# First pair of a ConvGLU as ordinary products, its operand sums in place, and the last four blocks in one down product

## The chip, the cores and the metric

The kernel runs on one core of a Trainium2 chip. The core has a matrix engine (TensorE; PE in the profile, its weight loads PEld), a vector engine (VectorE, DVE), a scalar engine (ScalarE, ACT), a general engine (GpSimd, POOL) and a sync engine (SyncE, SP) that here only issues transfers. Each engine takes its instructions from a queue of its own, in order. The metric is the device time of one execution in microseconds (us); lower is better. Before the change the median of three runs is 2178.03 us (2174.79 to 2182.94).

## The reference

One transformer encoder layer is applied to two requests that share the weights: a prompt of 1024 tokens and a sample of 512 tokens, each behind 16 learned meta tokens. The width D is 1024. All inputs and outputs are 32-bit floats.

```python
h = x + mixer(rms_norm(x))            # two kinds of attention heads, then w_out
n = rms_norm(h)                       # over the width, with a gain
gate = n @ w_ff_gate                  # 1024 x 2816
gate = pad[:, :-2] * conv_w[0] + pad[:, 1:-1] * conv_w[1] + pad[:, 2:] * conv_w[2] + conv_b   # over the tokens
h = h + (gelu(gate) * (n @ w_ff_up)) @ w_ff_down      # 2816 x 1024
y = rms_norm(h)[:, N_META:]
```

The change concerns the last three lines for the prompt (the ConvGLU and the final norm). The 2816 inner columns are 22 blocks of 128, and the kernel takes them two at a time, as 11 pairs.

## The kernel before

**Arithmetic.** Every product is made from three matmuls of a reduced float format (`mm3`, L129 to L133): an operand is split into a high part, rounded by ScalarE, and a low part, the difference, made by VectorE or GpSimd (`split`, L125 and L126); the three matmuls are high by high (L131), high by low (L132) and low by high (L133). All activations lie transposed, with the width on the 128 partitions and the tokens along the free dimension, so `h` is 8 tiles `h[:, k]`, one for each 128 of the width.

**Stages.** The program runs the projections, the attention of both requests, the sample's ConvGLU, and the prompt's output projection (`mixer_out`); the prompt's ConvGLU (`prompt_glu`) comes last, alone. Its matmuls begin at about 1417 us of the profile and it takes the remaining 760 us.

**The halves.** `prompt_glu` cuts the 1024 tokens into a left and a right half (H = 512 tokens, with a column of halo at each end: W = 514) and the width into an upper half (k = 0 to 3) and a lower half (k = 4 to 7). This gives four quarters of the normed input: b11 and b21 (left tokens), b12 and b22 (right tokens). A pair of gate or up blocks is then a 2 by 2 product of half matrices, and it is done with seven products in place of eight, by Strassen's method in Winograd's form (`products`, with `ORDER = 1, 2, 6, 7, 4, 5, 3`). Product 1 takes b11, 2 takes b21, 3 takes b22, and products 4 to 7 take sums of quarters: t1 = b12 - b11 (product 5), t2 = b22 - t1 (product 6), t3 = b22 - b12 (product 7) and t4 = b21 - t2 (product 4). These sums of the activations are made once, in the first pair, and each is split into a high and a low part (`put`). The weights of a pair need their own sums and splits each time (`strassen_weights`): two raw tiles come by transfers on SP's queue (L821), VectorE makes four sums in place (L836 to L841, one of them in a temporary `s`), ScalarE casts the seven high parts and GpSimd makes the seven low parts. The halves of the split weights are handed out in turn (`Halves`) from three pairs of tiles of 1024 columns (`w_hi`, `w_lo`, NW = 3); a tile is free again when the products of both of its halves are done. The raw tiles `w_f` are two (NRAW = 2).

**A pair.** The gate's seven products have 2 x 258 columns, and their results are combined on VectorE out of PSUM (L900); `gate_out` makes the convolution (L941, two VectorE steps L944) and the GELU (L946). The up's seven products have 512 columns; `up_out` multiplies by the gate (L953) and splits the result into `a_hi` and `ga` (the low part lies in a `ga` block). `down_all` multiplies the two blocks of the pair by `w_down` and adds the result to `h` on VectorE (L986): 8 width blocks by 2 halves of the tokens, each of six matmuls of 512 columns.

**The first pair.** When it begins, only the tokens of the first two of three chunks have their norm's factor `rstd`; the sum of squares of the last chunk is still being made on GpSimd (L619). So the first pair's gate is made of ordinary products (`dense`), left half first; the matmul that averages the last chunk's squares (L1011) follows behind the first of them, then `rstd` is finished, the right quarters are normed (L882) and split, and the right half of the gate follows. The sums t1 to t4 are then made from quarters that are normed once more into temporaries `tmp` (five buffers): 12 norms and 16 subtractions, a half of these on GpSimd (L886). The up's seven products follow. The first pair's gate weights are split with GpSimd's help (`load_weight` with `nc.gpsimd`).

**The end.** The last pair's down product is done in four chunks of 256 tokens: for each width block six matmuls of 256 columns, an add to `h` (L1096), a square (L618) and an add to the chunk's sum of squares on GpSimd (L619). While the next chunk runs, the chunk's mean is made by a matmul (L624), then `rs`, and `h` is scaled (L1083 on VectorE, L1080 and L1081 for each fourth) and stored. The last chunk sums its squares on TensorE (L1100) instead.

**What sets the order.** The program is traced in the order of the code, and a planner (`schedule_with_timeline_sim`) then orders each engine's queue by a simulated time line: an instruction that the simulation finds ready goes ahead of an earlier one that it finds waiting. A tile of a rotating tag waits until a buffer of the tag is free, and a tile of a later pool waits for the tiles whose memory it takes over.

## Time and profile before

| | before |
|---|---|
| median of three runs | 2178.03 us (2174.79 to 2182.94) |
| the profiled execution's own time | 2178.3 us |
| its span, first to last instruction | 2176.5 us |
| TensorE busy | 2062.9 us, 95% of the span |
| VectorE, ScalarE, GpSimd busy | 67%, 50%, 41% |
| mean granted TensorE clock | 0.981 |

The profile is one execution. "Busy" is the time in which an engine has an instruction under way; matmuls overlap each other, so that a row's duration (0.28 us for 258 columns) is more than the distance from one start to the next, and the distance is what a stream of matmuls costs. A row of the time line has the start, the duration, the engine, the line of the code, the operation, output and inputs, the shape and the number of merged instructions; in brackets stands how long the engine stood idle before it and what released it. A row of the windows has, for a stretch of time, the busy time and the number of instructions of each engine, the granted TensorE clock (1.00 is full speed), the share of the transfer engines and what they moved.

### The profile page before, as it was taken

The page shows a single profiled execution, that of the slowest core. Times are in us where ns is not written, and L with a number is a line of the kernel's source. Part 1 is how long each engine was busy: PE and PEld are TensorE (multiplying, and loading weights), DVE is VectorE, ACT ScalarE, POOL GpSimd, SP SyncE. Part 2 cuts the span into 40 slices and gives each one's busy share as a digit, 9 for nine tenths or more (in the row PEclk, how much of TensorE's full clock was granted, in tenths as well). Part 3 has the DMA queues.
Part 4 walks back from the last instruction along what each step waited for, and adds up shares of the span by engine and source line. Part 5 has one row for each costly group of instructions (what it writes and reads, how often), then busy time and mean ns, then how long its engine had stood idle before and what let it go on. Part 6 is the DMA issues. An engine that isn't in the chain of part 4 may idle for free.

```text
span 2176.5 us, 33391 instructions
## 1 busy us (share of the span) xinstructions
PE 2062.9 (95%) x12598; PEld 1853.3 (85%) x12598; DVE 1457.5 (67%) x2345; ACT 1083.4 (50%) x1970; POOL 900.2 (41%) x678
## 2 busy tenths in 40 slices
PE   7999999998999999999999999967999999999996
PEld 7898989986897888898889988965888888888885
DVE  7745565677758767667777777776665665666655
ACT  5534544567747445577777646532333222233333
POOL 5753345310132222344444313466544444445444
PEclk9999999999999999999999999988999999999998
DMA  6763455554233222233332227501111111111112
GB/s 228 223 214 111 140 166 161 166 188 130 73 89 91 86 78 82 87 104 101 124 108 77 70 75 242 169 29 39 59 59 49 49 46 52 58 39 59 58 40 78
DMA packets 112544, 222.84 MB, mean 102 GB/s; under 512 B 14464, under 2 KB 65920, under 8 KB 111872
## 3 DMA queue, kind: packets, MB, share of 16 engines
q1 hardware_dynamic: 92800, 149.40, 21.3%
q10 hardware_dynamic: 19584, 71.31, 10.0%
q8 instruction: 99, 1.62, 0.3%
q14 instruction: 61, 0.50, 0.1%
HBM read 172.11 MB, written 48.55 MB: 101 GB/s over the span
## 4 chain that ended last, share of the span: by engine, by line
PE 78%; DVE 9%; ACT 3%; POOL 3%; issue 3%; DMA 1%; ACTq 0%; DVEq 0%; POOLq 0%
PE ps_d L132 10%; PE ps_d L133 10%; PE ps_d L131 9%; PE ps_mm L131 9%; PE ps_mm L132 9%; PE ps_mm L133 9%; PE ps_t L466 5%; PE ps_s L445 3%; PE ps_s L446 3%; PE ps_o L481 2%; DVE p L449 2%; PE ps_o L480 1%; POOL w_lo L126 1%; DVE tmp L882 1%; PE ps_s L132 1%
## 5 line engine op out<-in xcount | busy, mean ns | idle before, releaser
L126 POOL TENSOR_TENSOR w_lo<-w_f,w_hi 128x512 fp32r<-128x512 f32 (+1 forms) x185 | 293.9, 1601 | 334.1 <-ACT w_hi L125 333.1
L131 PE MATMUL ps_mm<-xhi,w_hi 128*128 128x258 f32 (+4 forms) x1232 | 396.6, 322 | 2.6 <-DVE hn L117 2.5
L132 PE MATMUL ps_mm<-xlo,w_hi 128*128 128x258 f32 (+4 forms) x1232 | 392.1, 318 | 0.0
L133 PE MATMUL ps_mm<-xhi,w_lo 128*128 128x258 f32 (+4 forms) x1232 | 390.1, 317 | 0.0
L125 ACT CAST w_hi<-w_f 128x512 fp32r<-128x512 f32 (+1 forms) x219 | 160.4, 755 | 364.5 <-PE ps_d L132 279.1
L449 DVE TENSOR_SCALAR_CACHE_REDUCE p<-ps_s 128x1044 f32<-128x1044 f32 (+7 forms) x212 | 223.1, 1052 | 91.3 <-PE ps_s L446 76.5
L125 ACT CAST pt_hi<-ps_t 128x512 fp32r<-128x512 f32 (+8 forms) x360 | 170.3, 483 | 189.2 <-PE ps_t L466 174.1
L452 ACT ACTIVATE p<-p,nm 128x1040 f32<-128x1040 f32 (+7 forms) x212 | 215.2, 1015 | 92.0 <-DVE p L449 91.3
L131 PEld LDWEIGHTS ps_mm<-xhi,w_hi 128*128 128x128 f32 x1232 | 234.6, 191 | 12.9 <-DVE hn L117 3.1
L126 DVE TENSOR_TENSOR pt_lo<-ps_t,pt_hi 128x512 fp32r<-128x512 f32 (+6 forms) x312 | 172.8, 563 | 107.0 <-ACT pt_hi L125 106.0
L132 PEld LDWEIGHTS ps_mm<-xlo,w_hi 128*128 128x128 f32 x1232 | 234.4, 190 | 9.1 <-issue 0.5
L133 PEld LDWEIGHTS ps_mm<-xhi,w_lo 128*128 128x128 f32 x1232 | 234.4, 190 | 8.5 <-issue 0.2
L445 PE MATMUL ps_s<-k,q 128*128 128x348 f32 (+6 forms) x552 | 177.8, 328 | 17.8 <-DVE p L449 16.9
L900 DVE TENSOR_TENSOR tmp<-ps_d,tmp 128x512 f32<-128x512 f32 (+1 forms) x147 | 99.4, 687 | 133.5 <-PE ps_d L133 133.3
L466 PE MATMUL ps_t<-ident,p 128*128 128x128 f32 (+10 forms) x1188 | 181.9, 268 | 0.6 <-ACT r_rows L501 0.3
L446 PE MATMUL ps_s<-k,q 128*128 128x348 f32 (+6 forms) x552 | 170.7, 316 | 0.0
L466 PEld LDWEIGHTS ps_t<-ident,p 128*128 128x128 f32 (+10 forms) x1188 | 141.5, 135 | 29.4 <-issue 4.1
L151 POOL CAST w_hi<-w_f 128x1024 fp32r<-128x1024 f32 x66 | 70.8, 1081 | 218.0 <-issue 88.5
L986 DVE TENSOR_TENSOR h<-ps_d,h 128x1024 f32<-128x1024 f32 x80 | 97.7, 1222 | 85.7 <-PE ps_d L133 85.7
L132 PE MATMUL ps_d<-ga,w_hi 128*128 128x512 f32 x320 | 126.9, 397 | 0.9 <-POOL ga L126 0.9
L133 PE MATMUL ps_d<-a_hi,w_lo 128*128 128x512 f32 x320 | 126.8, 396 | 0.0
L445 PEld LDWEIGHTS ps_s<-k,q 128*128 128x128 f32 (+5 forms) x552 | 100.2, 182 | 31.0 <-DVE p L449 27.7
(312 smaller groups left out, 5462.2 us busy)
## 6 DMA issues: line engine op xcount, KB each, us to landing
w_f<-w_in ACTq DMA_DIRECT2D x36, 512.0 KB
w_f<-w_out ACTq DMA_DIRECT2D x32, 512.0 KB
q<-qk SPq DMA_DIRECT2D x48, 257.0 KB
w_f<-w_gate ACTq DMA_DIRECT2D x24, 512.0 KB
w_f<-w_up ACTq DMA_DIRECT2D x22, 512.0 KB
w_f<-w_down ACTq DMA_DIRECT2D x22, 512.0 KB
w_f<-w_up SPq DMA_DIRECT2D x22, 512.0 KB
w_f<-w_down SPq DMA_DIRECT2D x22, 512.0 KB
```

The lines of the kernel that those rows point to most:

```text
L125: return (nc.scalar.copy(hi, src), (lo_engine or nc.vector).tensor_tensor(out=lo, in0=src, in1=hi.bitcast(F32), op=ALU.subtract))
L126: (lo_engine or nc.vector).tensor_tensor(out=lo, in0=src, in1=hi.bitcast(F32), op=ALU.subtract))
L131: nc.tensor.matmul(ps, lhsT=whi, rhs=xhi, start=start, stop=False)
L132: nc.tensor.matmul(ps, lhsT=whi, rhs=xlo, start=False, stop=False)
L133: return nc.tensor.matmul(ps, lhsT=wlo, rhs=xhi, start=False, stop=stop).ins
L445: nc.tensor.matmul(ps[:, i], lhsT=q[0], rhs=kc, start=True, stop=False)
L446: nc.tensor.matmul(ps[:, i], lhsT=q[1], rhs=kc, start=False, stop=True)
L449: g.evicted = nc.vector.tensor_scalar(out=p.rearrange("p (i w) -> p i w", i=nch), in0=ps, scalar1=-HD ** -0.5, scalar2=3.0e38, op0=ALU.mul ...
L452: nc.scalar.activation(p, p, AF.Exp, bias=nm, scale=-1.0, accum_out=l)
L466: nc.tensor.transpose(tps[:, c:c + M], p[:, k0:k0 + kw], g.ident[:M, :M])
L900: nc.vector.tensor_tensor(out=o, in0=x, in1=y, op=ALU.add)
L986: nc.vector.tensor_tensor(out=hs, in0=d, in1=hs, op=ALU.add)
```

## The change

- **First pair.** Its up product becomes ordinary too: `gate_whole` and `up_whole` call `dense` on a whole half of the tokens. Three weights are loaded ahead on ScalarE's queue (two gate blocks and the first up block), the fourth behind the first right-hand gate; their low parts, and those of the quarters, are made on VectorE instead of GpSimd.
- **Sums.** The normed quarters are kept as floats (`f11`, `f21`, `f12`, `f22`) in the memory that t4, t2 and t3 take later. The 12 second norms are gone; the 16 subtractions are all on VectorE, two of each four in place. t1 and t4 are split as soon as they are made; t2 and t3 take over the tiles of b12, f12 and f22, so that they are split when the first pair's last products have read these. t3 is first copied by ScalarE.
- **Last four blocks.** The down product of the last pair but one isn't made in the loop; its activations are held, its two down weights are split into tiles of a late pool (in memory of t2 and t3), and the last stage adds four blocks at once, in the order 0, 1, 3, 2: 12 matmuls for each width block and chunk instead of six.
- **Memory.** `ga` has 8 buffers (5 before), `a_hi` 4 (2 before), and the memory reserved for dynamic transfers falls from its default of 16384 bytes of each partition to 1024, so that everything of the kernel that is laid out from that end moves by 15 KB.

The diff, cut to its core:

```diff
-def load_weight(g, src, lo_engine=None, hi_engine=None, wp=None):
+def load_weight(g, src, lo_engine=None, hi_engine=None):
...
-    ap = pool(ctx, g, "fa0", 2, "right")
+    ap = pool(ctx, g, "fa0", 4, "right")
...
-    b11f = parts(quarter(xp, "t4h", dt=F32))
-    b21f = [t[:, c:c + W] for t in [ap.tile([P, 2 * W], F32, name="b21f", tag="a_hi") for _ in range(2)] for c in (0, W)]
-    for i, nm in ((6, "t2"), (7, "t3")):
-        xs[i] = [parts(quarter(lp, nm + x)) for x in "hl"]
+    f11, f21 = [quarter(xp, nm, F32) for nm in ("t4h", "t4l")]
+    b12 = [quarter(lp, "t2" + x) for x in "hl"]
+    f12, f22 = [quarter(lp, nm, F32) for nm in ("t3l", "t3h")]
     def block():
-        return up.tile([P, H], F32, name="ga", tag="ga")
+        return up.tile([P, H], F32, name="ga", tag="ga", bufs=8)
...
-    def put(i, k, of, eng=None):
-        split(g, xs[i][0][k], xs[i][1][k], of, eng or nc.gpsimd)
+    def put(x, k, of, eng=None):
+        split(g, x[0][k], x[1][k], of, eng)
...
-    ws = [load_weight(g, g.w_gate[f], nc.gpsimd) for f in range(2)]
+    ws = [load_weight(g, w) for w in (g.w_gate[0], g.w_gate[1], g.w_up[0])]
+    gate, acts = new_gate(), new_acts()
+    gout, uout = gate_out(0, gate), up_out(gate, acts)
     ends = [c + w for c, w in token_chunks(0)]
     for c0, c1 in ((0, ends[0]), (ends[0], W)):
         for k in range(KT):
-            norm((b11f[k] if k < KH else b21f[k - KH])[:, c0:c1], k, c0, c1 - c0)
-    for k in range(KT):
-        put(1 + k // KH, k % KH, b11f[k] if k < KH else b21f[k - KH])
...
+            norm((f11[k] if k < KH else f21[k - KH])[:, c0:c1], k, c0, c1 - c0)
+    for k in range(KH):
+        put(xs[1], k, f11[k])
+    for k in range(KH):
+        put(xs[2], k, f21[k])
+    sides = [[xs[1][n] + xs[2][n] for n in range(2)], [b12[n] + xs[3][n] for n in range(2)]]
+    def gate_whole(i, x, between=None):
         ps = bank(2, W // 2 + 1)
         for n, (c0, cw) in enumerate(gcols):
+            dense(g, ps[:, n], ws[i], *sides[x], c0, cw)
+            if n == 0 and between:
+                between()
+        gout(i, x, ps)
+    def up_whole(i, x):
+        ps = bank(1, H)[:, 0]
+        dense(g, ps, ws[2 + i], *sides[x], 1, H)
+        uout(i, x, ps, temp([P, H]))
+    def fresh():
+        l0, lw, acc = st.last
+        mean = bank(1, lw)[:, 0]
+        nc.tensor.matmul(mean, lhsT=g.ones_d, rhs=acc, start=True, stop=True)
+        rsqrt_newton(g, None, rstd[:, l0:l0 + lw], mean, lw, y=st.y[:, :lw])
+        for f, x, k0 in ((f12, b12, 0), (f22, xs[3], KH)):
+            for k in range(KH):
+                norm(f[k], k0 + k, H, W)
+                put(x, k, f[k])
+    gate_whole(0, 0, fresh)
+    gate_whole(1, 0)
+    up_whole(0, 0)
+    gate_whole(0, 1)
+    ws.append(load_weight(g, g.w_up[1]))
+    gate_whole(1, 1)
+    up_whole(1, 0)
+    up_whole(0, 1)
+    up_whole(1, 1)
...
     for k in range(KH):
-        t12, t22, t11 = temp(), temp(), temp()
-        norm(t12, k, H, W)
-        norm(t22, k + KH, H, W)
-        norm(t11, k, 0, W)
...
-        sub(t1[k], t12, t11)
-        sub(t12, t22, t12, nc.gpsimd)
-        sub(t22, t22, t1[k])
-        sub(b21f[k], b21f[k], t22, nc.gpsimd)
-        put(6, k, t22, nc.vector)
-        put(7, k, t12)
...
+        t1, t4 = temp(), temp()
+        sub(t1, f12[k], f11[k])
+        sub(f12[k], f22[k], f12[k])
+        sub(f22[k], f22[k], t1)
+        sub(t4, f21[k], f22[k])
+        put(xs[5], k, t1, nc.gpsimd)
+        put(xs[4], k, t4)
+    for i, nm in ((6, "t2"), (7, "t3")):
+        xs[i] = [quarter(lp, nm + x) for x in "hl"]
     for k in range(KH):
-        put(4, k, b21f[k])
-    acts, lows = up_half(0, gate)
+        put(xs[6], k, f22[k])
+        t3 = temp()
+        nc.scalar.copy(t3, f12[k])
+        put(xs[7], k, t3, nc.gpsimd)
+    held = []
     for p in range(1, NFF // 2):
-        down_all(p - 1, acts, lows)
+        if p < NFF // 2 - 1:
+            down_all(p - 1, acts)
+        else:
+            held = acts
...
+    acts = held + acts
     late.close()
     op = pool(ctx, g, "fo0", 2, "left")
-    wd = down_weights(NFF // 2 - 1)
+    wd = []
+    for f in range(NFF - 4, NFF - 2):
+        tiles = [op.tile([P, D], F32R, name=nm, tag=nm) for nm in ("w_hi", "w_lo")]
+        wd.append([[t[:, c:c + D // 2] for t in tiles] for c in (0, D // 2)])
+        for w, r in zip(wd[-1], raw_weight(g, g.w_down[f])):
+            split(g, *w, r, nc.gpsimd)
+    wd += down_weights(NFF // 2 - 1)
...
-            down(ps, wd, acts, lows, j, c0, cw)
+            down(ps, wd, acts, (0, 1, 3, 2), j, c0, cw)
...
-    nc = bacc.Bacc("TRN2", target_bir_lowering=False, num_devices=1)
+    nc = bacc.Bacc("TRN2", target_bir_lowering=False, num_devices=1, dynamic_dma_scratch_size=1024)
```

More of the change, by code (lines that the diff above doesn't have):

```diff
@@ L148, in load_weight @@
     nc.scalar.dma_start(out=w, in_=src)
-    hi, lo = [(wp or g.wp).tile([P, D], F32R, name=nm, tag=nm, bufs=MW if wp else NW) for nm in ("w_hi", "w_lo")]
+    hi, lo = [g.wp.tile([P, D], F32R, name=nm, tag=nm, bufs=NW) for nm in ("w_hi", "w_lo")]
     if hi_engine:
@@ L947, in gate_out, with up_out, out, new_gate @@
         return out
-    def up_out(gate, acts, lows):
-        def out(i, x, src):
-            a = src[:, 0]
-            nc.vector.tensor_tensor(out=a, in0=a, in1=gate[i, x], op=ALU.mult)
-            lows[i, x] = block().bitcast(F32R)
-            split(g, acts[i][:, x * H:(x + 1) * H], lows[i, x], a, nc.gpsimd)
-        return out
+    def up_out(gate, acts):
+        def out(i, x, src, a=None):
+            a = src if a is None else a
+            nc.vector.tensor_tensor(out=a, in0=src, in1=gate[i, x], op=ALU.mult)
+            hi, lows = acts[i]
+            lows[x] = block().bitcast(F32R)
+            split(g, hi[:, x * H:(x + 1) * H], lows[x], a, nc.gpsimd)
+        return out
+    def new_gate():
+        return {(i, x): block() for i, x in ((0, 0), (1, 0), (1, 1), (0, 1))}
     def new_acts():
-        return [ap.tile([P, 2 * W], F32R, name="a_hi", tag="a_hi") for _ in range(2)]
+        return [(ap.tile([P, N], F32R, name="a_hi", tag="a_hi"), {}) for _ in range(2)]
     def down_weights(p):
@@ L996, in prompt_glu @@
         for k in range(KT):
-            norm((b11f[k] if k < KH else b21f[k - KH])[:, c0:c1], k, c0, c1 - c0)
-    for k in range(KT):
-        put(1 + k // KH, k % KH, b11f[k] if k < KH else b21f[k - KH])
-    gate = {}
-    out = gate_out(0, gate)
-    left = [xs[1][x] + xs[2][x] for x in range(2)]
-    for i in range(2):
+            norm((f11[k] if k < KH else f21[k - KH])[:, c0:c1], k, c0, c1 - c0)
[3 more added lines that the diff above has]
+        put(xs[2], k, f21[k])
@@ L1005, in prompt_glu @@
+    sides = [[xs[1][n] + xs[2][n] for n in range(2)], [b12[n] + xs[3][n] for n in range(2)]]
+    def gate_whole(i, x, between=None):
         ps = bank(2, W // 2 + 1)
         for n, (c0, cw) in enumerate(gcols):
-            dense(g, ps[:, n], ws[i], *left, c0, cw)
-            if i == n == 0:
-                l0, lw, acc = st.last
-                mean = bank(1, lw)[:, 0]
-                nc.tensor.matmul(mean, lhsT=g.ones_d, rhs=acc, start=True, stop=True)
-                rsqrt_newton(g, None, rstd[:, l0:l0 + lw], mean, lw, y=st.y[:, :lw])
@@ L1013, in prompt_glu @@
-        out(i, 0, ps)
-    b12 = [parts(quarter(xp, "t4" + x)) for x in "hl"]
-    xs[4] = b12
-    for k in range(KT):
-        t = temp()
-        norm(t, k, H, W)
-        put(4 if k < KH else 3, k % KH, t, nc.vector if k % 2 else nc.gpsimd)
-    fresh = [b12[x] + xs[3][x] for x in range(2)]
-    for i in range(2):
-        ps = bank(2, W // 2 + 1)
-        for n, (c0, cw) in enumerate(gcols):
-            dense(g, ps[:, n], ws[i], *fresh, c0, cw)
-        out(i, 1, ps)
-    t1a = parts(quarter(st.hp, "t1a", KH // 2))
@@ new lines, in prompt_glu @@
+    ws.append(load_weight(g, g.w_up[1]))
[3 more added lines that the diff above has]
+    up_whole(1, 1)
+    xs[5] = [[t[:, k] for t in [st.hp.tile([P, KH // 2, W], F32R, name=nm, tag=nm) for nm in ("t1a", "t1b")]
+              for k in range(KH // 2)], quarter(lp, "t1l")]
+    xs[4] = [quarter(xp, "t4" + x) for x in "hl"]
+    for k in range(KH):
+        t1, t4 = temp(), temp()
[5 more added lines that the diff above has]
+        put(xs[4], k, t4)
```

47 lines of the change are left out of this document (17 added, 30 removed).

## The prediction

> **What bounds the kernel now.** I read the page's totals first, then the windows by stage, then TensorE's time line where the windows show gaps.
>
> ```profile
> span 2176.5 us, 33391 instructions
> PE 2062.9 (95%) x12598; PEld 1853.3 (85%) x12598; DVE 1457.5 (67%) x2345; ACT 1083.4 (50%) x1970; POOL 900.2 (41%) x678
> ...
> 0.00:1417.00 1417.00, 1357.44 (x8625) 1236.40 (x8626) 978.19 (x1799) 835.22 (x1542) 520.44 (x384) 0.99 0.41 130
> 1417.00:1501.70 84.70, 50.95 (x286) 44.32 (x285) 62.56 (x62) 33.68 (x56) 62.26 (x45) 0.81 0.11 37
> 1501.70:2121.70 620.00, 620.00 (x3479) 540.70 (x3478) 384.47 (x420) 192.38 (x320) 293.48 (x220) 1.00 0.15 50
> 2121.70:2176.50 54.80, 34.51 (x214) 31.91 (x212) 32.31 (x66) 22.10 (x54) 24.02 (x31) 0.81 0.22 77
> ...
> 1456.20:1479.60 23.40, 0.00 (x0) 0.00 (x0) 21.77 (x20) 8.22 (x15) 15.68 (x12) 0.57 0.00 0
> 1507.40:1569.40 62.00, 62.00 (x350) 54.06 (x349) 37.74 (x43) 19.16 (x32) 30.18 (x22) 1.00 0.16 52
> ```
>
> TensorE is busy for 95% of the span, so the matmuls bound it, except in two places. From 1417 to 1501.7 it works 50.95 of 84.7 us at a clock of 0.81; from 2121.7 to the end 34.51 of 54.8 us, again at 0.81. Between them stand ten pairs, each exactly like 1507.4 to 1569.4: 62.0 of 62.0 us busy at full clock, VectorE 37.74, GpSimd 30.18. What the change does to work hidden behind those pairs costs nothing; what it does at the two ends counts in full. The time line says what TensorE waits for there:
>
> ```profile
> 1417.26 0.28 PE L131 MATMUL ps_d<-b11h,w_hi 128*128 128x258 f32 x1
> 1420.34 0.39 PE L133 MATMUL ps_d<-b11h,w_lo 128*128 128x258 f32 x1 [2.68 <-POOL w_lo L126]
> 1423.10 0.28 PE L131 MATMUL ps_d<-b11h,w_hi 128*128 128x258 f32 x1
> 1425.85 0.28 PE L133 MATMUL ps_d<-b21h,w_lo 128*128 128x258 f32 x1
> 1429.82 1.50 PE L1011 MATMUL ps_d<-t1a,ones_d 128*128 128x340 f32 x2 [3.69 <-POOL t1a L619]
> 1479.67 0.80 PE L131 MATMUL ps_d<-t2h,w_hi 128*128 128x512 f32 x1 [23.48 <-ACT w_hi L125]
> 1498.84 0.74 PE L131 MATMUL ps_d<-a_hi,w_hi 128*128 128x512 f32 x2 [2.99 <-ACT a_hi L125]
> 1563.69 0.63 PE L131 MATMUL ps_d<-a_hi,w_hi 128*128 128x512 f32 x2
> ...
> 2131.65 0.98 PE L624 MATMUL ps_mm<-acc,ones_d 128*128 128x256 f32 x2 [2.22 <-POOL acc L619]
> 2136.10 0.28 PE L133 MATMUL ps_mm<-a_hi,w_lo 128*128 128x256 f32 x1
> 2139.28 0.28 PE L133 MATMUL ps_mm<-a_hi,w_lo 128*128 128x256 f32 x1
> 2143.02 1.22 PE L624 MATMUL ps_mm<-acc,ones_d 128*128 128x256 f32 x2 [3.46 <-POOL acc L619]
> 2154.79 0.70 PE L1100 MATMUL ps_mm<-sq,ones_d 128*128 128x256 f32 x2 [4.12 <-ACT sq L1099]
> 2165.07 0.41 DVE L1096 TENSOR_TENSOR h<-ps_mm,h 128x256 f32<-128x256 f32 x1
> ```
>
> In the first pair it waits 2.68 us for GpSimd's low part of the first weight, 3.69 us for GpSimd's last sum of squares, 23.48 us while the sums and weights of the seven products are made, and 2.99 us for the activations of the down product. In the last stage it waits 2.22, 3.46 and 4.12 us at each chunk's mean: a chunk's matmuls are done before GpSimd's chain of sums, and the mean stands in TensorE's queue.
>
> **Durations of a matmul in a stream.** 258 columns: from 1423.10 to 1425.85 are 24 starts, 2.75 / 23 = 0.120 us. 256 columns: from 2136.10 to 2139.28 are 28, 3.18 / 27 = 0.118 us. 512 columns: a pair has 96 of them for down and 84 for up beside 168 of 258 for the gate, so (62.0 - 168 x 0.120) / 180 = 0.2325 us.
>
> **The first pair.** A pair in the steady stretch begins its down product at 1563.69; one period of 62.0 us earlier, 1501.7, is where the first pair's down begins as the rest of the program sees it. From the first matmul at 1417.26 that is 84.4 us. After the change the work is 192 matmuls of the gate (23.0 us) and 96 of the up (22.3 us, 12 more than the seven products' 84, so +2.8 us), 45.3 us, and 0.8 us for the mean's matmul: from 1429.82 the next starts at 1430.6. If nothing else were lost, 46.1 us.
>
> What could be lost, in order. (1) The first wait: the first weight's low part now goes to VectorE, and its queue also gets eight low parts of the left quarters, in the place where GpSimd had them.
>
> ```profile
> 1417.46 0.51 DVE L680 TENSOR_TENSOR h<-ps_s,res 128x340 f32<-128x340 f32 x1 [3.21 <-PE ps_s L133]
> 1427.54 1.27 DVE L837 TENSOR_TENSOR w_f<-w_f 128x512 f32<-128x512 f32 x1
> 1434.14 5.49 DVE L882 SCALAR_TENSOR_TENSOR tmp<-h,gain,t1b 128x514 f32<-128x514 f32 x5
> 1448.76 0.69 DVE L886 TENSOR_TENSOR tmp<-tmp 128x514 f32<-128x514 f32 x1
> 1477.25 1.72 DVE L838 TENSOR_TENSOR tmp<-w_f 128x512 f32<-128x512 f32 x1
> 1428.87 0.90 POOL L619 TENSOR_TENSOR t1a<-t1a,sq 128x340 f32<-128x340 f32 x1 [0.60 <-ACT sq L618]
> 2111.94 1.29 POOL L126 TENSOR_TENSOR w_lo<-w_f,w_hi 128x512 fp32r<-128x512 f32 x1
> 2118.74 0.62 ACT L125 CAST w_hi<-w_f 128x512 fp32r<-128x512 f32 x1 [0.53 <-PE ps_d L132]
> 1428.30 0.49 ACT L618 ACTIVATE sq<-h 128x340 f32<-128x340 f32 x1 [3.03 <-POOL t1a L619]
> 1420.32 3.35 DMA w_f<-w_up
> L882 DVE SCALAR_TENSOR_TENSOR tmp<-h,gain,t1b 128x514 f32<-128x514 f32 x20 | 23.0, 1184 | 0.2
> L886 DVE TENSOR_TENSOR tmp<-tmp 128x514 f32<-128x514 f32 x8 | 9.6, 1204 | 1.5 <-POOL tmp L886 1.2
> L944 DVE SCALAR_TENSOR_TENSOR ga<-ps_d,vec,ga 128x512 f32<-128x512 f32 x8 | 5.9, 743 | 0.7 <-ACT ga L941 0.7
> L986 DVE TENSOR_TENSOR h<-ps_d,h 128x1024 f32<-128x1024 f32 x80 | 97.7, 1222 | 85.7 <-PE ps_d L133 85.7
> L619 POOL TENSOR_TENSOR acc<-acc,sq 128x256 f32<-128x256 f32 x21 | 15.8, 755 | 9.7 <-ACT sq L618 8.9
> q1 hardware_dynamic: 92800, 149.40, 21.3%
> q10 hardware_dynamic: 19584, 71.31, 10.0%
> ```
>
> One such VectorE operation takes 0.69 us alone (the row at 1448.76). Eight are 5.5 us, and VectorE is idle for 3.21 us just before 1417.46 alone; I cost this at nothing; without that cover, a TensorE wait of the old kind, 2.7 us. (2) The last sum of squares: GpSimd's queue holds no low parts there any more. The last add to `h` starts at 1417.46; add 0.5 us for it, a square of 0.49 and a sum of 0.90 (the rows at 1428.30 and 1428.87), and the mean can start at 1419.4; the code puts it behind 24 matmuls, at 1420.2. So that wait goes. (3) The right quarters: from the mean's start to the first norm took 4.3 us (1429.82 to 1434.14). First norm then 1424.5; eight norms and eight low parts at 0.68 are 10.9 us, and in the same queue stand four convolution steps of 0.74, an up weight's low part (two of 0.69) and a multiplication (0.7), 5 us: the last right quarter is there at about 1440.4. TensorE has the left half to do first, 2 x 5.8 + 5.6 + 0.8 = 18.0 us, so it comes to the right half at 1435.3 and to its last quarter tile 2.5 us later: 2.6 us late. (4) A short loss of clock behind that: none to 1 us. I take 3 us in all, 49 us for the stage, and 35.4 us gained; 38.3 at best.
>
> Then the sums. They no longer stand ahead of the up product, but t2 must be ready when product 6 of the second pair's gate starts: 22.3 us of down product and two gate products of 2.9 us behind it, at 1417.3 + 49 + 28 = 1494. VectorE has, from 1424 on, 44 operations with two inputs in SBUF (8 norms, 8 + 8 low parts, 16 subtractions, 4 weight sums), two weights' low parts (2.8 us), eight convolution steps (5.9), four multiplications (2.8) and eight adds to `h` of 1.22 (9.8). Alone that is 44 x 0.69 + 21.3 = 52 us of 70. But beside a busy GpSimd the same operations took 1.18 and 1.20 us in the mean (L882 and L886): 44 x 1.2 + 21.3 = 74 us, 4 us too many. GpSimd has about 20 operations of 1.3 us there, 26 of 70 us, where it was busy 62.26 of 84.7; so the truth lies nearer the first end, about 60, and it fits. Planned queues leave small waits; I take 3 us, between nothing and 10. Gain of the first pair: 32.4 us.
>
> [...]
>
> **The last stage.** Before, 54.8 us from 2121.7. After: 32 times 12 matmuls of 256 columns, 384 x 0.118 = 45.3 us; three means and eight sums of squares on TensorE, pairs of short matmuls of 0.70 us alone (the row at 2154.79) and about half of that in a stream, 11 x 0.35 = 3.8 us as an estimate; from the last matmul the last add can follow in 0.4 us, and from that add at 2165.07 to the end of the span are 11.4 us as now. 60.9 us. The loop loses one down product, 96 x 0.2325 = 22.3 us: net 38.6, a gain of 16.2 us. The means' waits vanish since a chunk's matmuls last 11.3 us and its eight sums on GpSimd 8 x 0.755 = 6.0 us. The eight adds to `h` that go were hidden and pay nothing. What is new: four down weights pass through two raw tiles. The third transfer can start when the first weight's two halves are split, the fourth behind the second's; a transfer takes 3.35 us, a high part 0.62, a low part 1.29. The held weights' tiles come free with product 6, third of seven, of the last up: four products of 12 x 0.2325 = 2.8 us, 11 us, before its end; two halves are split 3.5 us later, the third weight lands at -4, the fourth at -2, its low part is made behind the others about 2 us after the end. Between nothing, if TensorE does the held blocks of several tiles first, and 5 us with a cold clock; I take 3. Gain 13.2 us.
>
> **Weight tiles in the loop.** With no seven products in the first pair the halves are handed out from another start: a down weight now fills one tile, and its second-used tile is free only behind product 4, fifth of seven, two products or 5.6 us before the down needs it. A split needs 0.62 + 1.29 and its turns in two queues; I cost that at nothing, with the rest of the 5.6 us as cover.
>
> **Memory.** Both busy transfer queues (q1 and q10, of SP and ACT) are of the hardware kind and GpSimd issues no transfer, so the smaller reserve itself costs nothing. But the earlier stages' tiles move, and waits for memory taken over move with them. TensorE's idle time before 1417 is 1417 - 1357.4 = 59.6 us; I take nothing, with 6 us to both sides, a tenth of it, as an estimate.
>
> **The sum.** 2176.5 - 32.4 - 13.2 = 2130.9; the profiled execution lasted 1.8 us beyond its span (2178.3), and the runs' median is 0.3 us below that execution: 2132 us.
>
> **Rivals.** A: VectorE is late with the sums, because it and GpSimd hold each other up (1.2 us rows); product 6 waits up to 10 us in place of 3, and the matmuls behind run some 2 us slower: 2141. For it: VectorE was busy 21.77 of 23.4 us in the present gap. Against it: 12 norms fewer, and half the work on GpSimd. B: the sums are not made meanwhile, since their temporaries take turns with the up's in five buffers: the weight sum at 1477.25 had its input at 1428.8 and waited for a buffer. Then they start with the down product: 16 subtractions, 8 low parts and 4 weight sums at 0.69 to 1.2 us and 9.8 us of adds are 29 to 43 us, where there are 28; 2143 if it is 14 us late in place of 3. C: the last stage waits for the fourth weight and cold matmuls follow, gain there 5 us instead of 13.2: 2140. D, slower: the new start of the halves makes each of nine down products wait for the late tile. It decides from 45.6 / 9 = 5.1 us a pair: 5.6 us of lead would have to become a delay of 5; at 5.5 us the time is 2182. Against it: GpSimd idles half of each pair (30.18 of 62.0). E: the ordinary up and the new ends gain as forecast, but earlier stages lose more than 6 us by moved memory: 2145.
>
> **Chances.** Forecast 0.50, own range 2121 to 2143; A 0.16, B 0.08, C 0.13, E 0.07, D 0.06. The low end is 2123, with nothing lost (38.3 + 16.2 us), less 6 for moved memory: 2117. The high end must hold A, B, C and most of E and of two of them together: 2160. A measurement of this kernel can tell about 0.5% (11 us) from no change. All cases but D, and a D at half its price (0.05 for the bound), are faster by more: 0.90, within 0.05, slower 0.05.
>
> **What would show it.** Right: the first down matmul about 35 us earlier against its period; no wait over 3 us between the first gate matmul and it; periods of 62.0 us; L624 without an idle entry; L886 on VectorE only, at 0.7 to 0.9 us. Wrong: idle entries at product 6's first matmul released by ACT or DVE (A, B), by POOL `w_lo` in the last stage (C), or in each period (D).

## The result, and the profile after

The changed kernel takes 2145.47 us (median of four runs, 2144.5 to 2146.14) against 2177.34 us (median of four, 2174.79 to 2182.94): a ratio of 0.985, 95% interval 0.983 to 0.987. It is faster by 31.9 us, where 46 were forecast. The time is 13.5 us above the predicted 2132 us. It lies inside the wide range of 2117 to 2160, whose high end was there to hold the rivals, and just outside the 2121 to 2143 that the forecast itself allowed; the case whose mechanism the runs below show is rival B, priced at 2143. The profiled execution's span of 2142.5 us lies 11.6 us above the forecast's 2130.9.

The page's first line of the changed kernel, and its windows by stage (columns as before: stretch, its length, busy time and number of instructions of PE, PEld, DVE, ACT and POOL, granted clock, share of the transfer engines, GB/s):

```profile
span 2142.5 us, 33530 instructions
...
0.00:1418.30 1418.30, 1360.77 (x8626) 1239.80 (x8627) 981.34 (x1808) 837.08 (x1544) 515.71 (x379) 0.99 0.41 130
1418.30:1464.60 46.30, 46.30 (x292) 41.63 (x291) 23.05 (x33) 20.27 (x31) 11.10 (x9) 1.00 0.19 65
1464.60:1486.67 22.07, 22.07 (x97) 18.01 (x96) 21.73 (x24) 5.99 (x10) 8.82 (x6) 1.00 0.01 4
1486.67:1508.00 21.33, 12.47 (x85) 12.26 (x84) 16.01 (x17) 10.76 (x20) 11.87 (x9) 0.76 0.00 1
...
1539.24:2078.20 538.96, 538.62 (x3035) 468.92 (x3035) 349.40 (x370) 169.09 (x285) 268.20 (x193) 1.00 0.15 50
2078.20:2142.50 64.30, 51.40 (x407) 49.29 (x405) 32.24 (x66) 25.17 (x58) 33.46 (x38) 0.96 0.24 83
```

The first pair's own products (second stretch) run without any gap: 46.30 of 46.30 us busy, where before 50.95 of 84.7 were. The gap has moved and shrunk: it now lies behind the down product, from 1486.67 to 1508, where TensorE works 12.47 of 21.33 us at a clock of 0.76. VectorE tells why. In the second stretch it is busy 23.05 of 46.30 us; in the third, beside the down product, 21.73 of 22.07. The work that was to be done in the first of these is done in the second. The time lines of TensorE and VectorE of the changed kernel show it:

```profile
1464.64 0.39 PE L131 MATMUL ps_d<-a_hi,w_hi 128*128 128x512 f32 x1
1501.46 0.58 PE L131 MATMUL ps_d<-t2h,w_hi 128*128 128x258 f32 x1 [8.86 <-ACT w_hi L125]
1501.84 0.42 PE L132 MATMUL ps_d<-t2l,w_hi 128*128 128x258 f32 x1
...
1506.14 0.34 PE L133 MATMUL ps_d<-t3h,w_lo 128*128 128x258 f32 x1
...
2086.12 0.39 PE L131 MATMUL ps_mm<-a_hi,w_hi 128*128 128x256 f32 x1 [1.62 <-ACT w_hi L125]
```

```profile
1438.40 0.74 DVE L944 SCALAR_TENSOR_TENSOR ga<-ps_d,vec,ga 128x512 f32<-128x512 f32 x1
1445.67 1.23 DVE L126 TENSOR_TENSOR w_lo<-w_f,w_hi 128x1024 fp32r<-128x1024 f32 x1 [6.53 <-ACT w_hi L125]
...
1456.60 0.69 DVE L953 TENSOR_TENSOR tmp<-ps_d,ga 128x512 f32<-128x512 f32 x1 [5.45 <-PE ps_d L133]
1459.26 0.69 DVE L953 TENSOR_TENSOR tmp<-ps_d,ga 128x512 f32<-128x512 f32 x1 [1.97 <-PE ps_d L133]
1464.91 0.69 DVE L953 TENSOR_TENSOR tmp<-ps_d,ga 128x512 f32<-128x512 f32 x1 [4.96 <-PE ps_d L133]
1465.51 1.67 DVE L885 TENSOR_TENSOR tmp<-t3l,t4h 128x514 f32<-128x514 f32 x1
...
1475.79 1.21 DVE L991 TENSOR_TENSOR h<-ps_d,h 128x1024 f32<-128x1024 f32 x1
...
1495.53 0.70 DVE L885 TENSOR_TENSOR tmp<-t4l,t3h 128x514 f32<-128x514 f32 x1 [0.46 <-DVE t3h L885]
...
1499.10 1.66 DVE L841 TENSOR_TENSOR tmp<-w_f 128x512 f32<-128x512 f32 x1
```

The quarters are normed and split by 1438; from then to 1464.9 VectorE stands idle for 6.53, 5.45, 1.97 and 4.96 us, waiting for a weight's high part and for ups. The first subtraction (L885) starts directly behind the multiplication of the last of the four ups, at 1465.51. From there the 16 subtractions, eight low parts and three weight sums share VectorE with the adds to `h` (L991, 1.21 us each) until 1499; the weight sum of product 6 (L841) is the last of them, and product 6 waits 8.86 us for it. Behind the wait, from 1501.46 to 1506.14, the granted clock is 0.50 and the matmuls of 258 columns come every (1506.14 - 1501.84) / 20 = 0.215 us instead of 0.120: 22 of them lose 2.1 us.

The last stage takes 64.30 us against 60.9 + 3. Two waits are left in it: 1.62 us for a weight's high part (last row of TensorE's time line above) and 1.13 us at the last sum of squares. The means no longer stop TensorE (group of the changed kernel's L627; the last number is the idle time ahead of it):

```profile
L627 PE MATMUL ps_mm<-acc,ones_d 128*128 128x256 f32 x12 | 3.6, 384 | 0.0
```

The steady pairs differ in a place that the forecast had not in view. One pair before, and its up alone; then the same after:

```profile
1563.69:1625.66 61.97, 61.97 (x349) 54.04 (x348) 37.44 (x42) 19.29 (x33) 30.18 (x23) 1.00 0.16 52
1606.12:1625.66 19.54, 19.54 (x86) 15.82 (x85) 12.52 (x16) 9.08 (x17) 12.87 (x10) 1.00 0.26 82
```

```profile
1601.60:1663.96 62.36, 62.36 (x349) 54.13 (x348) 40.18 (x42) 18.97 (x33) 31.00 (x22) 1.00 0.16 51
1644.15:1663.96 19.81, 19.81 (x86) 15.83 (x85) 12.90 (x15) 6.91 (x13) 12.33 (x9) 1.00 0.29 92
```

TensorE is busy throughout and at full clock in both, and yet a pair takes 0.39 us longer, 0.27 of it in the up's 84 matmuls of 512 columns: 0.2358 us each instead of 0.2326.

**Where the 11.6 us went.** The third pair's down product, at 1601.60, is the first that stands in the steady stretch; two steady periods ahead of it is 1601.60 - 2 x 62.36 = 1476.88. From the first gate matmul (1418.32) to there are 58.6 us; the forecast had 49 + 3.

| term | forecast, us | in the span, us | difference |
|---|---|---|---|
| first gate matmul | 1417.3 | 1418.3 | +1.1 |
| first pair's own products | 49 | 46.3 | -2.7 |
| waits and slow matmuls behind it (sums) | 3 | 58.6 - 46.3 = 12.3 | +9.3 |
| nine pairs, and one gate and up | 9 x 62.0 + 39.7 = 597.7 | 2078.20 - 1476.88 = 601.3 | +3.6 |
| last stage | 63.9 | 64.3 | +0.4 |

Of the 12.3 us behind the first pair, 8.86 are the wait at product 6 and 2.1 the slow matmuls. The other 1.3 lie in the second pair's up and down products, among them waits of 0.46 us for a temporary and 0.34 us for a low part. The first row is within the scatter: in the profiles of this case the first gate matmul stands anywhere from 1416.4 to 1421.2 us.

### The profile page after: what moved, and what is told of

Its sections match the earlier page's. It is cut to its first block, busy times and chain, and to the rows that moved or that the text cites. A ratio compares the mean times of both kernels' runs of the same rounds, so it can differ in the third digit from the quotient of the medians.

```text
span 2142.5 us, 33530 instructions
## 1 busy us (share of the span) xinstructions
PE 2062.4 (96%) x12706; PEld 1856.0 (87%) x12706; DVE 1447.9 (68%) x2342; ACT 1082.2 (51%) x1968; POOL 869.7 (41%) x645
## 4 chain that ended last, share of the span: by engine, by line
PE 80%; DVE 8%; ACT 3%; issue 3%; POOL 2%; DMA 1%; ACTq 0%; DVEq 0%; POOLq 0%
PE ps_mm L131 10%; PE ps_mm L132 10%; PE ps_mm L133 10%; PE ps_d L133 9%; PE ps_d L132 9%; PE ps_d L131 9%; PE ps_t L469 5%; PE ps_s L448 4%; PE ps_s L449 3%; DVE p L452 2%; PE ps_o L484 2%; PE ps_o L483 2%; PE ps_s L133 1%; POOL w_lo L126 1%; PE ps_s L132 1%
## 5 line engine op out<-in xcount | busy, mean ns | idle before, releaser
L899 DVE TENSOR_TENSOR tmp<-ps_d,tmp 128x516 f32<-128x516 f32 (+1 forms) x140 | 94.7, 688 | 104.4 <-PE ps_d L133 101.9
L991 DVE TENSOR_TENSOR h<-ps_d,h 128x1024 f32<-128x1024 f32 x72 | 87.1, 1219 | 60.9 <-PE ps_d L133 60.9
L126 POOL TENSOR_TENSOR w_lo<-tmp,w_hi 128x512 fp32r<-128x512 f32 x40 | 53.0, 1325 | 165.2 <-PE ps_d L132 126.1
L582 POOL TENSOR_TENSOR p<-p 114x1040 f32<-114x1040 f32 (+2 forms) x33 | 80.9, 2450 | 84.4 <-ACT p L581 84.3
```

The source lines that it names most:

```text
L126: (lo_engine or nc.vector).tensor_tensor(out=lo, in0=src, in1=hi.bitcast(F32), op=ALU.subtract))
L899: nc.vector.tensor_tensor(out=o, in0=x, in1=y, op=ALU.add)
L991: nc.vector.tensor_tensor(out=hs, in0=d, in1=hs, op=ALU.add)
```

## Experiments

Two theories stood for the late sums. **B**, a rival of the prediction: the sums' temporaries take turns with the temporaries of the ups in the five `tmp` buffers. **A**, another: VectorE and GpSimd hold each other up, whatever the order. Two more questions were the longer pair and what each part is worth alone. Three kernels take parts of the change alone, and nine vary the changed kernel; each was run beside the kernel before, whose median was 2177.3 to 2179.8 us.

### The sums traced ahead of the ups

```diff
     gate_whole(1, 1)
+    for k in range(KH):
+        t1, t4 = temp(), temp()
+        sub(t1, f12[k], f11[k])
...
     up_whole(1, 0)
     up_whole(0, 1)
     up_whole(1, 1)
-    for k in range(KH):
-        t1, t4 = temp(), temp()
-        sub(t1, f12[k], f11[k])
...
```

> The changed kernel with one edit: the loop that makes the sums t1 to t4 stands in the code ahead of the last three ups of the first pair (behind the last gate) instead of behind them; same instructions, same buffers. Theory B (the sums are late because their two temporaries come after the ups' temporaries in the turn of the five buffers): first subtraction on VectorE at about 1440 us instead of 1465.5, no wait over 1 us at product 6 of the second pair's gate (8.86 now), no slow matmuls behind it (2.2 us now), time 2134 us, 11 less than the changed kernel's 2145.5. Theory A (VectorE and GpSimd hold each other up, whatever the order): the wait stays over 5 us, time 2142 to 2147.

Measured: 2137.44 us (2134.02 to 2138.18), ratio 0.9813 (0.9799 to 0.9826). Product 6 does not wait. The sums start at 1436.5, but a new wait stands in the down product, where an add to `h` has got behind the low parts of t2 in VectorE's queue (VectorE's and then TensorE's time line of this run):

```profile
1436.48 0.68 DVE L885 TENSOR_TENSOR tmp<-t3l,t4h 128x514 f32<-128x514 f32 x1
...
1461.07 6.71 DVE L126 TENSOR_TENSOR t2l<-t3h,t2h 128x514 fp32r<-128x514 f32 x4 [0.87 <-ACT t2h L125]
```

```profile
1472.33 0.50 PE L131 MATMUL ps_d<-a_hi,w_hi 128*128 128x512 f32 x1 [2.52 <-DVE h L991]
```

The order alone brings 8 of the 11 us; most of the 3 us short is this wait. A falls as the cause.

### The up without a temporary

```diff
-        uout(i, x, ps, temp([P, H]))
+        uout(i, x, ps, gate[i, x])
```

> The changed kernel with one edit: the first pair's up is multiplied in place into its gate's block, so that it takes no temporary; the order of the code is the changed kernel's. Theory B: the same as when the sums are traced ahead, 2134 us, first subtraction at about 1440 us, no wait over 1 us at product 6. If it is the place in the code that decides and not the buffers: 2145 and the first subtraction behind the last up at 1465. Theory A: wait over 5 us, 2142 to 2147.

Measured: 2135.26 us (2135.11 to 2135.4), ratio 0.9806 (0.9792 to 0.9819). VectorE's time line, and the windows of the first pair and of the first down product with the second pair:

```profile
1433.64 0.69 DVE L885 TENSOR_TENSOR tmp<-t3l,t4h 128x514 f32<-128x514 f32 x1
1440.18 0.68 DVE L885 TENSOR_TENSOR t3l<-t3h,t3l 128x514 f32<-128x514 f32 x1
...
1460.73 0.68 DVE L885 TENSOR_TENSOR tmp<-t4l,t3h 128x514 f32<-128x514 f32 x1
```

```profile
1419.66:1465.98 46.32, 46.32 (x293) 41.60 (x292) 42.56 (x55) 29.31 (x48) 17.57 (x12) 1.00 0.17 55
1465.98:1529.90 63.92, 62.95 (x349) 53.81 (x348) 43.92 (x44) 20.55 (x36) 38.12 (x27) 1.00 0.16 54
```

The code's order is the changed kernel's; only the four temporaries of the ups are gone. All 16 subtractions are now done between 1433.6 and 1461.4, among the ups, and VectorE is busy 42.56 of 46.32 us in the first pair (23.05 in the changed kernel) without holding TensorE up. B holds: it was the temporaries. The first sum's temporary is the fifth of five buffers, so no buffer was occupied; that a temporary is handed out only after those that stand before it in the code is the reading that fits, and it was not tried by itself.

### The smaller reserve alone

```diff
-    nc = bacc.Bacc("TRN2", target_bir_lowering=False, num_devices=1)
+    nc = bacc.Bacc("TRN2", target_bir_lowering=False, num_devices=1, dynamic_dma_scratch_size=1024)
```

> The kernel before with the reserve for dynamic transfers of 1 KB alone, so that the memory laid out from that end moves by 15 KB. If the move makes a pair's period 62.35 us instead of 62.0 and the start of the ConvGLU 1 us later, as in the changed kernel: 2177.3 + 10 x 0.35 + 1 = 2182 us. If these come from the other edits: 2177 within 1 us and a period of 62.0.

Measured: 2180.97 us (11 runs, 2176.54 to 2183.68) against 2178.75 us (15 runs): ratio 1.0012 (1.0003 to 1.002). The pairs take 61.97 us as before, so the longer pair does not come from the reserve. 0.7 to 4.4 us are lost all the same, in a place that stays open: the first gate matmul is at 1421.13 in this profile, but in the profiles of kernels whose code ahead of it is the same it was seen from 1416.4 to 1421.2.

### The last four blocks alone, and the first pair alone

First the kernel before with the last group, its buffers and the reserve:

```diff
-    ap = pool(ctx, g, "fa0", 2, "right")
+    ap = pool(ctx, g, "fa0", 4, "right")
-        return up.tile([P, H], F32, name="ga", tag="ga")
+        return up.tile([P, H], F32, name="ga", tag="ga", bufs=8)
...
-        down_all(p - 1, acts, lows)
+        if p < NFF // 2 - 1:
+            down_all(p - 1, acts, lows)
+        else:
+            held, hlows = acts, lows
...
-            down(ps, wd, acts, lows, j, c0, cw)
+            down(ps, wd, acts, lows, j, c0, cw, (0, 1, 3, 2))
```

> The kernel before with the last four blocks in one group, the eight ga and four a_hi buffers and the reserve that they need, but with the first pair as before. By the changed kernel's trace the last stage (64.3 us against 54.8 + 22.3) gains 12.8 us: 2164.5 us, or 2168 if the longer period of 62.35 us comes with this part's memory. If the stage's gain needed the first pair's change: 2170 or more.

Measured: 2170.01 us (2166.64 to 2171.44), ratio 0.9962 (0.9947 to 0.9977). The gain is 8.7 us, or 11.0 against the kernel with the reserve alone, which it contains. Its steady pairs take 62.01 to 62.13 us, so the longer pair does not come with this part.

Then the changed kernel with the down product of the last pair but one back in the loop:

```diff
-        if p < NFF // 2 - 1:
-            down_all(p - 1, acts)
-        else:
-            held = acts
+        down_all(p - 1, acts)
...
-            down(ps, wd, acts, (0, 1, 3, 2), j, c0, cw)
+            down(ps, wd, acts, (1, 0), j, c0, cw)
```

> The changed kernel without its last group: the down product of the last pair but one is made in the loop again and the last stage adds two blocks; two a_hi buffers. It has the late sums of the changed kernel. If the parts add up, and the last group gains 12.8 us as in the changed kernel's trace: 2145.5 + 12.8 = 2158 us; if it gains only the 8.7 us that the kernel before gained from it: 2154. A period of 62.36 us here shows that the longer period belongs to the first pair's edits; 62.0 that it belongs to the last group's buffers.

Measured: 2154.85 us (2154.26 to 2155.79), ratio 0.9897 (0.9882 to 0.9912), with pairs of 62.36 us, and the wait of 8.84 us at product 6. The first pair brings 22.4 us, and the last group 2154.85 - 2145.47 = 9.4 us on top of it. So the last group is worth 9 to 11 us, and not the 12.9 that the two profiles give (55.0 + 22.2 against 64.3). The base of that comparison is one execution's last stage. Here it is, chunk by chunk, in the kernel before, and then the same code in the run with the reserve alone:

```profile
2121.50:2131.65 10.15, 7.94 (x67) 7.73 (x65) 6.41 (x13) 5.63 (x15) 7.77 (x10) 1.00 0.00 1
2131.65:2143.02 11.37, 7.90 (x50) 7.55 (x51) 8.15 (x16) 5.20 (x13) 6.66 (x9) 0.81 0.21 73
2143.02:2154.79 11.77, 7.65 (x39) 7.26 (x39) 6.86 (x14) 5.25 (x13) 6.53 (x9) 0.75 0.23 80
2154.79:2176.50 21.71, 11.22 (x60) 9.57 (x60) 10.89 (x23) 6.21 (x15) 3.07 (x4) 0.76 0.32 112
```

```profile
2128.15:2138.28 10.13, 7.93 (x67) 7.73 (x66) 6.41 (x13) 5.61 (x15) 7.76 (x10) 1.00 0.00 0
2138.28:2147.86 9.58, 6.36 (x50) 6.10 (x51) 7.80 (x16) 4.98 (x13) 6.87 (x9) 0.95 0.26 90
2147.86:2158.90 11.04, 7.57 (x39) 7.18 (x39) 7.31 (x14) 5.25 (x13) 6.66 (x9) 0.74 0.30 107
2158.90:2179.00 20.10, 9.62 (x60) 8.10 (x60) 10.88 (x23) 6.09 (x15) 3.06 (x4) 0.79 0.31 109
```

The same instructions take 55.0 us in the one and 50.9 in the other, and 53.5 in the run with the first pair alone, whose last stage adds two blocks too: at the waits for the means the clock falls (in the kernel before it was 1.00 ahead of the first, and 0.50 from 2131.94 to 2135.35, from 2142.18 to 2149.00 and from 2155.83 to 2159.24), and for how long differs from one execution to the next (0.81 and 0.95 in the second chunk, behind waits of 2.22 and 2.20 us). Of these three the profile of before has the longest.

### The longer pair: where the quarters begin, and which half comes first

In the kernel before, the four k of a quarter lie in one tile, 2056 bytes apart; in the changed kernel each has a tile of its own:

```diff
-    def quarter(p, tag, k=KH, dt=F32R):
-        return p.tile([P, k, W], dt, name=tag, tag=tag)
...
+    def quarter(p, tag, dt=F32R):
+        return [p.tile([P, W], dt, name=tag, tag=f"{tag}{k}") for k in range(KH)]
```

The up reads its 512 columns from column 1, which is 4 bytes on. If a tile begins at a multiple of 32 bytes, a matmul's moving operand (the activations that it streams) starts at 4, 12, 20 and 28 modulo 32 bytes for k = 0 to 3 before, and at 4 for nearly every k after (the high parts of t1 still lie two in a tile). The profile shows no addresses, but its distances fit, if not in the order of the starts: averaged over the ups of the steady pairs, the three matmuls of one k come every 0.235, 0.231, 0.234 and 0.230 us for k = 0 to 3 before, and every 0.235 to 0.236 us for all four k after. Three runs, all with the up without a temporary. The first gives the tiles the four starts back:

```diff
-        return [p.tile([P, W], dt, name=tag, tag=f"{tag}{k}") for k in range(KH)]
+        return [p.tile([P, W + 6], dt, name=tag, tag=f"{tag}{k}")[:, 2 * k:2 * k + W] for k in range(KH)]
```

> The version whose first-pair up takes no temporary, with one more edit: each quarter's tile for k is six columns wider and its data begin at column 2k, so that the columns start 8k bytes behind a tile's start, as they do modulo 32 bytes in the kernel before, where the four k of a quarter lie in one tile. If the longer period (62.36 against 61.97 us) comes from the quarters' alignment: a period of 62.0 and 2135.3 - 3.5 = 2132 us. If not: 62.36 and 2135.3.

The second puts all at 28 (but for the high parts of t1):

```diff
-        return [p.tile([P, W], dt, name=tag, tag=f"{tag}{k}") for k in range(KH)]
+        return [p.tile([P, W + 6], dt, name=tag, tag=f"{tag}{k}")[:, 6:6 + W] for k in range(KH)]
```

> The version whose first-pair up takes no temporary, with each quarter's tile six columns wider and its data beginning at column 6 for every k, so that the up's 512 columns start at 28 modulo 32 bytes everywhere (at 4 in the changed kernel). In the run with offsets of 2k the up's matmuls came every 0.235 us at k = 0 (start at 4) and every 0.228 at k = 3 (start at 28). If the start decides: an up of 84 x 0.228 = 19.2 us instead of 19.81, a period of 61.7 and 2135.3 - 10 x 0.65 = 2129 us. If only the mixing of starts over k helped: 62.36 and 2135.

The third shifts the halves instead, by one line ahead of the loop over the pairs:

```diff
     held = []
+    halves.next()
     for p in range(1, NFF // 2):
```

> The version whose first-pair up takes no temporary, with one more edit: one half of a weight tile is passed over before the loop, so that the halves are handed out from the same start as in the kernel before. If the longer period comes from the halves' start (the prediction's rival D in small): a period of 62.0 and 2132 us. If not: 62.36 and 2135.3.

Measured: the windows of a pair and of its up, first with the four starts, then with all at 28, then with the other half first (there with the down product between them):

```profile
1591.68:1653.72 62.04, 62.04 (x349) 54.11 (x348) 40.53 (x42) 18.89 (x33) 31.10 (x22) 1.00 0.15 52
...
1634.19:1653.72 19.53, 19.53 (x86) 15.83 (x85) 13.08 (x15) 6.81 (x13) 12.39 (x9) 1.00 0.28 91
```

```profile
1588.14:1649.90 61.76, 61.76 (x349) 54.02 (x348) 40.58 (x42) 18.92 (x32) 31.05 (x22) 1.00 0.16 52
...
1630.62:1649.90 19.28, 19.28 (x86) 15.76 (x85) 13.07 (x15) 6.80 (x12) 12.33 (x9) 1.00 0.29 95
```

```profile
1588.12:1650.40 62.28, 62.28 (x350) 54.12 (x349) 38.56 (x42) 19.15 (x33) 29.18 (x23) 1.00 0.16 52
1588.12:1610.32 22.20, 22.20 (x98) 18.02 (x97) 13.48 (x13) 2.21 (x4) 6.05 (x5) 1.00 0.08 24
1630.58:1650.40 19.82, 19.82 (x87) 15.84 (x86) 12.54 (x17) 9.06 (x17) 12.93 (x10) 1.00 0.26 81
```

| run | time, us | pair, us | up, us |
|---|---|---|---|
| up without a temporary (starts at 4) | 2135.26 | 62.36 | 19.81 |
| starts at 4, 12, 20, 28 | 2132.54 (2130.62 to 2135.11) | 62.04 | 19.53 |
| starts at 28 | 2128.72 (2124.09 to 2130.18) | 61.76 | 19.28 |
| other half first | 2133.09 (2130.52 to 2134.87) | 62.28 | 19.82 |

The times of the first, second and fourth row cannot be told apart: the intervals of their ratios (0.9792 to 0.9819, 0.9779 to 0.9811, 0.9782 to 0.9817) overlap. The windows can, since a steady pair takes the same time to 0.01 us from one to the next within each of these runs.

The start decides: 0.2358 us for a matmul that starts at 4, 0.2295 at 28, and with the old mixture of starts the old 0.2325. With all at 28, the averages for the four k are 0.228 to 0.231 us; with the four starts, in the run below that has them and all else together, they are 0.236 at k = 0 and 0.229 at k = 3 (the second expectation had 0.235 and 0.228). The quarters' tiles explain 0.32 us of the 0.39 of a pair, and the halves' start 0.08, each by its own run; the latter lies in the down product and the gate and not in the up. Why the halves' start matters to the matmuls was not tried. The pair with all starts at 28 is shorter than the kernel before's.

The run with the other half first has its time from another place than expected. From the first gate matmul to the last stage it is 2.3 us shorter than the run without that line, and eight steady pairs account for only 0.6 us of them. The other 1.6 us are the pair of the first down product: 62.30 us without a wait, where it was 63.92 with 1 us of waits.

### The wait in the last stage, and all together

```diff
-def raw_weight(g, src):
-    w = g.wp.tile([P, D], F32, name="w_f", tag="w_f", bufs=NRAW)
+def raw_weight(g, src, wp=None):
+    w = (wp or g.wp).tile([P, D], F32, name="w_f", tag="w_f", bufs=NRAW)
...
-    wd += down_weights(NFF // 2 - 1)
+    wd += down_weights(NFF // 2 - 1, op)
```

> The version whose first-pair up takes no temporary, with one more edit: the raw tiles of the last two down weights lie in the late pool, so that four raw tiles stand behind four weights in place of two. If the 1.6 to 2.2 us wait at the third weight comes from the two raw tiles (rival C): the wait goes and the time is 2133 us, against 2135.3. If ScalarE's and GpSimd's splits set it: wait and time stay.

Measured: 2132.63 us (2130.92 to 2135.67). The wait for a high part becomes a shorter one for GpSimd's low part (TensorE's time line with the up without a temporary, and then with the own raw tiles too):

```profile
2076.89 0.38 PE L131 MATMUL ps_mm<-a_hi,w_hi 128*128 128x256 f32 x1 [2.22 <-ACT w_hi L125]
```

```profile
2079.38 0.39 PE L133 MATMUL ps_mm<-a_hi,w_lo 128*128 128x256 f32 x1 [1.27 <-POOL w_lo L126]
```

The raw tiles were a part of it, 1 us, and GpSimd's splits behind them the rest. The time alone does not show a gain (ratio 0.9796, 0.9779 to 0.9813, against 0.9806, 0.9792 to 0.9819).

The weight that TensorE waits for is the last of the four to be loaded. In the changed kernel ScalarE casts the third weight's halves from 2082.38 us and the fourth's from 2085.45, and the matmul starts at 2086.12. The order 0, 1, 3, 2 takes the fourth weight third, ahead of one that is split earlier; in the run with own raw tiles GpSimd likewise makes the third weight's low parts first. The order 0, 1, 2, 3 was not run.

All together, with the quarters from column 6 or from column 2k:

```diff
-            split(g, *w, r, nc.gpsimd)
-    wd += down_weights(NFF // 2 - 1)
+            split(g, *w, r)
+    wd += down_weights(NFF // 2 - 1, op)
```

> All that helped, on the version whose first-pair up takes no temporary: quarters from column 6, one half passed over, own raw tiles for the last two down weights, and the low parts of the two held weights on VectorE instead of GpSimd. If the parts add up: 2129 (quarters) less 10 x 0.08 (half) less 2 (last stage) = 2126 us; if GpSimd still sets the wait in the last stage, 2128.

> The same with the quarters from column 2k instead of 6. If the parts add up: 2135.3 - 3.2 (quarters) - 0.8 (half) - 2 (last stage) = 2129 us, and slower than with column 6 by the difference of the two ups, 10 x 0.33 us, if the start decides.

And the first of these two with GpSimd back in its place:

```diff
-            split(g, *w, r)
+            split(g, *w, r, nc.gpsimd)
```

> The version with all that helped and the quarters from column 6, with the low parts of the two held weights on GpSimd again. On VectorE they made TensorE wait 2.63 us near the start of the last stage (64.5 us); with own raw tiles and GpSimd's low parts the stage took 63.3 us and the wait was 1.27. If the two engines' places in that stage add up: 2125.85 - 1.2 = 2124.7 us. If the last stage is set elsewhere: 2126.

Measured: 2125.85 us (2123.01 to 2126.79) with starts at 28, 2128.32 us (2124.59 to 2130.18) with the four starts, and 2122.62 us (2120.41 to 2123.74) with starts at 28 and the held weights' low parts on GpSimd again. The terms of the first sum did not come as counted, though the 2126 did. Its steady pairs take 61.58 us, 0.18 below those with starts at 28 alone, where 0.08 were counted for the half; the pair of its first down product is 1.1 us shorter than there; and its last stage takes 64.46 us, no less than with the up without a temporary (64.33). On VectorE the held weights' low parts made TensorE wait earlier (TensorE's time line of the first of the three):

```profile
2060.01 0.39 PE L133 MATMUL ps_mm<-a_hi,w_lo 128*128 128x256 f32 x1 [2.63 <-DVE w_lo L126]
```

With them on GpSimd the last stage takes 63.48 us. That they belong there is read from this wait; the ratios' intervals of the two versions (0.9742 to 0.9771 and 0.972 to 0.976) overlap. The last version has a ratio of 0.974 (0.972 to 0.976) to the kernel before, where the changed kernel has 0.985 (0.983 to 0.987): it beats both. Its windows of the first pair, the first down product with the second pair, the rest of the pairs and the last stage:

```profile
1418.76:1464.45 45.69, 45.69 (x292) 41.47 (x291) 41.94 (x55) 29.01 (x47) 16.89 (x12) 1.00 0.15 49
1464.45:1526.14 61.69, 61.69 (x349) 53.98 (x348) 40.97 (x44) 21.40 (x37) 36.00 (x28) 1.00 0.17 58
1526.14:2058.32 532.18, 532.18 (x3037) 468.08 (x3036) 329.99 (x370) 170.89 (x285) 261.83 (x192) 1.00 0.16 53
2058.32:2121.80 63.48, 51.02 (x407) 49.28 (x405) 31.14 (x66) 24.89 (x58) 33.53 (x38) 0.95 0.19 67
```

From the first gate matmul to the last stage TensorE does not wait at all.

## Why the prediction was right or wrong

**Right: what the change buys at the first pair.** The 23.48 us of waiting ahead of product 6 and the three smaller waits are gone. Points (1), (2) and (4) held: no wait at the first weight, none at the mean, no lost clock. Point (3), the right quarters 2.6 us late, did not happen: in a stream the low parts came every 0.62 us, the last was made at 1437.9, and TensorE waited for none of them (VectorE's time line of the changed kernel):

```profile
1432.31 2.50 DVE L126 TENSOR_TENSOR t2l<-t3l,t2h 128x514 fp32r<-128x514 f32 x4
...
1435.99 1.89 DVE L126 TENSOR_TENSOR b22l<-t3h,b22h 128x514 fp32r<-128x514 f32 x3
```

So the pair's products took 46.3 us, where the bare sum was 46.1 and 3 us of waits were taken.

**Wrong: "Planned queues leave small waits; I take 3 us" for the sums.** This is the step that failed: 12.3 us stand in the span where it put 3 (and 10 at most), 9.3 of the 11.6 us. VectorE's work was counted and fits, as forecast: in the run without the ups' temporaries it is done in time, beside a first pair in which VectorE is busy 42.56 of 46.32 us. What was not followed to the end was the order. Rival B named the mechanism and its sign (the temporaries take turns with the up's, so that the sums start with the down product), and it is what happened: it put 14 us in place of the 3, and 12.3 were measured, of which the wait of 8.9 us and the 2.1 us of slow matmuls are 11. It was given 0.08. That the time fell inside the range is owed to the room made there for rivals, and not to the forecast. The prediction had the evidence in hand: a weight sum of the kernel before that stood from 1428.8 to 1477.25, by its own reading waiting for a temporary, and the up of the change takes a temporary each time.

**Rival A** was not the cause. VectorE's two-input operations did slow down beside GpSimd (1.67 us at 1465.51, while GpSimd made low parts from 1465.34 to 1471.8, against 0.68 us at 1473.98, while it stood idle until 1476.0), which lengthened the sums once they were late; moved forward, they were just as exposed (the 16 subtractions take 15.0 us in the run without the ups' temporaries and 15.2 us in the changed kernel), and TensorE lost 1.0 us behind them (62.95 of 63.92 us busy in that run).

**Wrong: "Weight tiles in the loop ... at nothing", and the pair of 62.0 us.** The forecast looked for waits and found none, rightly; rival D's stall did not come. But 3.6 us went into matmuls that are each a little slower. The layout of the quarters, one tile for each k instead of four in one, stood in the diff and was not costed at all: 0.32 us a pair. The halves' start costs the other 0.08, for a reason that stays open.

**The last stage.** The forecast of 60.9 us with 3 us for the weights behind the two raw tiles came out at 64.3, with 1.62 us at the weight that is loaded last (rival C's mechanism, below its price) and 1.13 us at the last sum of squares. The gain was still smaller than the 13.2 us of the sum, 9 to 11 us. The base of 54.8 us was one execution in which the clock was low for long; 50.9 and 53.5 us in two others would lower the gain by about 4 and 1.5 us.

**Memory.** Taken as nothing, with 6 us to both sides; the reserve alone cost 0.7 to 4.4 us, rival E in small, in a place that was not found. That the smaller reserve itself costs nothing, by the kind of the transfer queues, was the author's inference: no run shows it apart from the memory that moves.

## What to carry to other kernels

Before costing moved work as hidden, follow what it must take in turn with the work it is to overtake: a shared rotating temporary holds back an instruction whose inputs and engine are both free, and the cure can be one line: multiplying in place here gained 10 us, and moving the code 8. When tiles are cut differently, compare the distance from start to start of the matmuls that read them, not only the waits; and where a stage runs at a changing clock, take its time from more than one execution (the same last stage took 50.9 to 55.0 us here).
